# A decoder trunk in split float32 on one core: activations held still and weights moved 512 wide, with PE transposes between

## The chip, the cores and the metric

The kernel runs on one core of one Trainium2 chip. The metric is the device time of one execution in microseconds, from the first to the last instruction of the core with what the runtime measures around them; three runs of the kernel before are given, and one execution of it was taken with the hardware profiler. TensorE is written PE here, its weight loads PEld, VectorE DVE, ScalarE ACT, GpSimd POOL and SyncE SP, as in the profile.

## The reference

256 tokens of width 2048 pass through two layers. Every sublayer computes `h = h + RMSNorm_post(f(RMSNorm_pre(h)))`. With all gains and norms written `n()`:

```python
# layer 0
proj = n(h) @ w_in                        # 2048 x 6144: xin | C | B
h = h + n((B * conv3(C * xin)) @ w_out)   # causal depthwise convolution, width 3
h = h + n(square(relu(n(h) @ w_up0)) @ w_down0)      # 2048 x 8192, 8192 x 2048
K, V = split(n_kv(h) @ w_kv)              # 2048 x 4096, 16 heads of 128
# layer 1: stick-breaking attention, strictly causal, then the same MLP
z = q k / sqrt(128);  A = exp(log_sigmoid(z) + sum of log(1 - sigmoid(z)) over later keys)
h = h + n((A @ V) @ w_o)
h = h + n(square(relu(n(h) @ w_up1)) @ w_down1)
```

All inputs and the output are float32. The weights are 402.7 MB, which at 128 x 128 numbers a tile is 6144 tiles: 768 in `w_in`, 256 each in `w_out`, V, K, Q and `w_o`, 1024 in each half MLP matrix (up or down).

## The kernel before

**Precision.** PE multiplies in a reduced float32 format (`F32R`). Each operand is therefore split into a high part, rounded by an ACT copy, and a low part, the difference, made by DVE. A product is hi x hi + hi x lo + lo x hi.

**Layout.** Activations are kept transposed: features on partitions, the 256 tokens along a row. A weight tile of 128 x 128 is the stationary operand. `mm` (L211) needs two matmuls for a tile: the high part of the weights against 512 columns (256 tokens high, 256 tokens low, L218), and the low part against 256 columns (L219). The two halves of the 512-wide PSUM bank are added later by `combined` (L236: an ACT copy and a DVE add). In the last output column of a sublayer (`direct`, L213 to L217) three matmuls of 256 columns take their place, so that no such addition is needed at the end.

**Order.** `product` runs over the 16 (or 32) feature tiles of one output column; `products_lead` runs 6 or 7 output columns side by side at the start of a sublayer, so that PE can begin as soon as the first feature tile is ready. The V projection alone is done the other way (L497 to L511): the activations are stationary, the weights move 512 wide, in three matmuls for each pair (L509, L510, L511).

**Weights.** `load_one` brings chunks of 8 tiles (512 KB) on SP's queue into 4 buffers; `split_one` splits a chunk with one ACT copy (L173) and one DVE subtraction (L175) into one of 3 buffers for each part. 768 chunks are used in a fixed order; a chunk is split two ahead of its use.

**Between sublayers.** The sum of squares is gathered as tiles appear (`Squares`). At the end, `rstd_soon` (L294) makes the reciprocal root: matmuls with `pick` (L299), ACT square root (L304), DVE reciprocal and two diagonal matrices (L309), and matmuls that spread it over partitions (L313). Then `residual` (L342: L351, L353) updates `h` tile by tile, and `split_scaled` (L245: L247, L248) makes the next operand. PE can do nothing in that time, because the norm covers all 2048 features of a token.

**Attention.** Heads go in pairs. For each head there are float32 products: `scores` (L539, L540), the cumulative sums in `weights` (L572 to L577, in F32R), and `mixed` (L589, L590). They are placed by hand between the K and Q products of the following heads (L608 to L620). ACT has to load a function table when it changes between exp and log (L534). PSUM banks are given out in turn from one pool of 8.

The Tile framework's scheduler orders the instructions of each engine by priority, and inserts the semaphores.

Of the kernel before, what the change touches and what calls it, by code (L numbers as in the profile page):

```python
# [14 lines left out]
P = 128  # L15
D = 2048
T = 256
KD = D // P
FF = 4 * D
NF = FF // P  # L20
# [3 lines left out]
LEAD_UP = 7  # L24
CH = 8
FIRST = 2


def lead_then_rows(n_tiles, k_tiles, lead):
    """Order of weight tiles: the first `lead` columns k by k, the others column by column."""  # L30
    order = [(k, n) for k in range(k_tiles) for n in n_tiles[:lead]]
    order += [(k, n) for n in n_tiles[lead:] for k in range(k_tiles)]
    return order


IN_N = [j * KD + i for i in range(KD) for j in range(3)]
HALF = NF // 2

ORDERS = {
    "in": lead_then_rows(IN_N, KD, LEAD),  # L40
    "out": lead_then_rows(list(range(KD)), KD, LEAD),
    "v": [(k, KD + 8 * g + n) for g in range(2) for k in range(KD) for n in range(8)],
    "kq": [(k, n) for n in range(KD) for k in range(KD)],
    "wo": lead_then_rows(list(range(KD)), KD, LEAD),
    "up0": lead_then_rows(list(range(HALF)), KD, LEAD_UP),
    "up1": lead_then_rows(list(range(HALF, NF)), KD, 0),
    "dn0": [(k, n) for n in range(KD) for k in range(HALF)],
    "dn1": [(k, n) for n in range(KD) for k in range(HALF, NF)],
}

G_MIX0, G_POST0, G_MLP0, G_MPOST0, G_KV, G_MIX1, G_POST1, G_MLP1, G_MPOST1, G_C0, G_C1, G_C2 = range(12)
# [3 lines left out]
def trunk(ctx, tc, xT, vecs, ws, outT):  # L55
    nc = tc.nc
    const = ctx.enter_context(tc.tile_pool(name="const", bufs=1))
    res = ctx.enter_context(tc.tile_pool(name="res", bufs=KD // 2))
    act = ctx.enter_context(tc.tile_pool(name="act", bufs=48))
    wpool = ctx.enter_context(tc.tile_pool(name="w", bufs=4))  # L60
    wsplit = ctx.enter_context(tc.tile_pool(name="ws", bufs=3))
    tmp = ctx.enter_context(tc.tile_pool(name="tmp", bufs=3))
    psum = ctx.enter_context(tc.tile_pool(name="ps", bufs=8, space=bass.MemoryType.PSUM))

    gv = const.tile([P, 12, KD], F32, name="gv")
    nc.scalar.dma_start(gv[:], vecs.rearrange("p (g k) -> p g k", g=12))

    def g(i, k):
# [6 lines left out]
    pick = const.tile([P, 3], F32, name="pick")  # L75
    nc.vector.memset(pick[:], 0.0)
    nc.vector.memset(pick[:, 1:2], 1.0 / D)
    ones = const.tile([P, P], F32, name="ones")
    nc.vector.memset(ones[:], 1.0)
    later = const.tile([P, P], F32, name="later")  # L80
    nc.gpsimd.affine_select(
        out=later[:], in_=ones[:], pattern=[[-1, P]], compare_op=ALU.is_gt,
        fill=0.0, base=0, channel_multiplier=1,
    )
    causal = const.tile([P, P], F32, name="causal")
    nc.gpsimd.affine_select(
        out=causal[:], in_=ones[:], pattern=[[1, P]], compare_op=ALU.is_gt,
        fill=0.0, base=0, channel_multiplier=-1,
    )

    ident = const.tile([P, P], F32, name="ident")
    nc.gpsimd.affine_select(
        out=ident[:], in_=ones[:], pattern=[[1, P]], compare_op=ALU.is_equal,
        fill=0.0, base=0, channel_multiplier=-1,
    )
# [6 lines left out]
    def bank(name):  # L102
        return psum.tile([P, 512], F32, tag="ps", name=name)

    def small(tag, name=None, bufs=3, cols=T):
        return tmp.tile([P, cols], F32, tag=tag, name=name or tag, bufs=bufs)

    # ---- weights: a stream of chunks of CH tiles, each split exactly into two parts
    stream = []

    class Weights:
        def __init__(self, name, ap):
            self.ap, self.order = ap, ORDERS[name]
            self.at = {kn: i for i, kn in enumerate(self.order)}
            self.n = ap.shape[0]
            self.got = {}
            stream.extend((self, c) for c in range(self.n))

        def parts(self, k, n):
            i = self.at[(k, n)]  # L120
            ahead((self, i // CH))
            hi, lo = self.got[i // CH]
            return hi[:, i % CH, :], lo[:, i % CH, :]

        def wide(self, k, n):
            i = self.at[(k, n)]
            ahead((self, i // CH))
            hi, lo = self.got[i // CH]
            j = i % CH
            return (  # L130
                hi[:, j : j + 4, :].rearrange("p a b -> p (a b)"),
                lo[:, j : j + 4, :].rearrange("p a b -> p (a b)"),
            )

    state = {"loaded": 0, "split": 0, "limit": 1 << 30, "order": (None, None)}
    raw = {}

    def load_one():
        i = state["loaded"]
        if i >= len(stream):  # L140
            return
        w, c = stream[i]
        t = wpool.tile([P, CH, P], F32, tag="raw", name=f"raw{i}")
        n = CH // 2 if i < FIRST else CH
        for a in range(0, CH, n):
            nc.sync.dma_start(
                t[:, a : a + n, :], w.ap[c, :, a * P : (a + n) * P].rearrange("p (a b) -> p a b", a=n)
            )
        raw[i] = t
        state["loaded"] += 1  # L150

    def after(ins):
        return nullcontext() if ins is None else tc.issue_after(ins.ins)

    def urgent(w):
        return tc.high_priority() if w in kq.values() else nullcontext()

    def split_one():
        hi_after, lo_after = state["order"]
        i = state["split"]  # L160
        if i >= len(stream):
            return
        while state["loaded"] <= i:
            load_one()
        w, c = stream[i]
        t = raw.pop(i)
        hi = wsplit.tile([P, CH, P], F32R, tag="hi", name=f"whi{i}")
        lo = wsplit.tile([P, CH, P], F32R, tag="lo", name=f"wlo{i}")
        n = 2 if i < FIRST else CH
        for a in range(0, CH, n):  # L170
            at = slice(a, a + n)
            with after(hi_after), urgent(w):
                nc.scalar.activation(hi[:, at, :], t[:, at, :], AF.Copy)  # L173
            with after(lo_after), urgent(w):
                nc.vector.tensor_tensor(lo[:, at, :], t[:, at, :], hi[:, at, :].bitcast(F32), op=ALU.subtract)  # L175
        w.got[c] = (hi, lo)
        state["split"] += 1
        load_one()

    done = set()  # L180

    def ahead(key):
        if key in done:
            return
        done.add(key)
        i = stream.index(key)
        while state["split"] <= min(i + 2, state["limit"]) and state["split"] < len(stream):
            split_one()

    def hold(name):  # L190
        """Until the next norm is under way, split no more than two chunks after this phase."""
        state["limit"] = max(i for i, (w, _) in enumerate(stream) if w is W[name]) + 2

    W = {}
    sequence = ["in", "out", "up0_0", "dn0_0", "up1_0", "dn1_0", "v", "kq", "wo",
                "up0_1", "dn0_1", "up1_1", "dn1_1"]
    kq = {}
    for name in sequence:
        base = name[:3] if name[:2] in ("up", "dn") else name
        if name == "kq":  # L200
            K = Weights("kq", ws["k"])
            Q = Weights("kq", ws["q"])
            del stream[-2 * K.n :]
            for c in range(K.n):
                stream.extend([(K, c), (Q, c)])
            kq["k"], kq["q"] = K, Q
        else:
            W[name] = Weights(base, ws[name])

    # ---- building blocks  # L210
    def mm(ps, w, x, first, last, direct=False):  # L211
        hi, lo = w
        if direct:  # L213
            nc.tensor.matmul(ps[:, :T], hi, x[:, :T], start=first, stop=False)  # L214
            nc.tensor.matmul(ps[:, :T], hi, x[:, T:], start=False, stop=False)  # L215
            nc.tensor.matmul(ps[:, :T], lo, x[:, :T], start=False, stop=last)  # L216
            return  # L217
        nc.tensor.matmul(ps[:], hi, x[:], start=first, stop=False)  # L218
        nc.tensor.matmul(ps[:, :T], lo, x[:, :T], start=False, stop=last)  # L219

    def product(w, xs, n, ks, direct=False):
        ps = bank("acc")
        for i, k in enumerate(ks):
            mm(ps, w.parts(k, n), xs[k], i == 0, i == len(ks) - 1, direct)
        return ps

    def products_lead(w, xs, ns, ks, before=None):
        pss = [bank("lead") for _ in ns]
        for i, k in enumerate(ks):
            if before is not None:  # L230
# [469 lines left out]
```

## Time and profile before

| | |
|---|---|
| Time, median of 3 runs | 2214.81 us (2212.7, 2214.81, 2215.17) |
| Span of the profiled execution | 2212.8 us; no time of its own is given beside the span |
| Mean granted PE clock | 0.993 |
| PE busy | 99% of the span, 12492 matmuls |
| DVE, ACT busy | 65%, 51% |
| DMA | 409.04 MB, 185 GB/s |

Busy time of PE is modelled, and neighbouring matmuls overlap in it: a share of 99% says that PE always had a matmul in flight, not that it was at its peak. The pace is read from the starts of neighbouring matmuls. A row of a group gives: line, engine, operation, tiles, shapes, count, then busy us, mean ns of one, idle time before and its releasers.

### The profile page before, as it was taken

What the parts mean: (1) busy time and instruction counts of PE and PEld (TensorE: products, weight loads), DVE (VectorE), ACT (ScalarE), POOL (GpSimd) and SP (SyncE); (2) the same over time, 40 slices, a digit from 0 to 9 for tenths busy, and PEclk for the clock granted to TensorE, in tenths of its full rate; (3) what the DMA queues carried; (4) which work ended last, traced back from release to release, by engine and by line L of the source; (5) the groups of instructions that cost most, each with busy time, mean ns of one, the idle gap of its engine ahead of it and who ended that gap; (6) DMA issues with size and microseconds to landing.
All of it is one profiled execution on the core that took longest, in us unless ns stands there. A gap on an engine that the chain in (4) does not pass through costs nothing.

```text
span 2212.8 us, 31971 instructions
## 1 busy us (share of the span) xinstructions
PE 2180.2 (99%) x12492; PEld 1910.6 (86%) x12492; DVE 1440.5 (65%) x2100; ACT 1119.9 (51%) x1630; POOL 1.0 (0%) x7
## 2 busy tenths in 40 slices
PE   8999999999999999999999999999999999999997
PEld 7888888888888888888888888888888888888886
DVE  7766656977444677655675777669775446776555
ACT  6444455544444444444465666656544444444442
POOL 0000000000000000000000000000000000000000
PEclk9999999999999999999999999999999999999998
DMA  6555554555555555555455444445555555555553
GB/s 240 191 190 190 191 190 162 190 191 190 190 190 191 189 191 189 191 189 190 167 190 182 163 164 163 167 163 190 190 190 190 190 190 190 189 190 190 190 189 120
DMA packets 113480, 409.04 MB, mean 185 GB/s; under 512 B 12592, under 2 KB 12720, under 8 KB 113328
## 3 DMA queue, kind: packets, MB, share of 16 engines
q1 hardware_dynamic: 112608, 405.85, 54.1%
q8 instruction: 98, 1.61, 0.3%
q10 hardware_dynamic: 720, 1.15, 0.1%
q14 instruction: 54, 0.44, 0.1%
HBM read 404.85 MB, written 2.10 MB: 184 GB/s over the span
## 4 chain that ended last, share of the span: by engine, by line
PE 98%; DVE 1%; ACT 0%; DMA 0%; issue 0%; ACTq 0%; DVEq 0%
PE acc L218 55%; PE acc L219 28%; PE lead L218 6%; PE lead L219 3%; PE accv L509 1%; PE accv L511 1%; PE accv L510 1%; PE acc L216 1%; PE acc L214 1%; PE acc L215 1%; PE z L539 0%; DVE x L353 0%; PE o L589 0%; DVE upd L351 0%; DMA gv<-vecs 0%; PE ex L572 0%
## 5 line engine op out<-in xcount | busy, mean ns | idle before, releaser
L218 PE MATMUL acc<-u,whi 128*128 128x512 f32 x5136 | 1786.3, 393 | 0.0
L219 PE MATMUL acc<-u,wlo 128*128 128x256 f32 x5136 | 1429.9, 278 | 0.0
L175 DVE TENSOR_TENSOR wlo<-raw,whi 128x1024 fp32r<-128x1024 f32 (+1 forms) x774 | 940.7, 1216 | 710.2 <-ACT whi L173 709.5
L173 ACT ACTIVATE whi<-raw 128x1024 fp32r<-128x1024 f32 (+1 forms) x774 | 814.7, 1053 | 1002.4 <-PE acc L218 486.1
L218 PEld LDWEIGHTS acc<-u,whi 128*128 128x128 f32 x5136 | 962.2, 187 | 218.6
L219 PEld LDWEIGHTS acc<-u,wlo 128*128 128x128 f32 x5136 | 966.6, 188 | 0.2
L218 PE MATMUL lead<-u,whi 128*128 128x512 f32 x416 | 151.5, 407 | 10.9 <-ACT whi L173 6.6
L219 PE MATMUL lead<-u,wlo 128*128 128x256 f32 x416 | 119.0, 286 | 0.0
L218 PEld LDWEIGHTS lead<-u,whi 128*128 128x128 f32 x416 | 81.4, 196 | 30.0 <-ACT whi L173 6.6
L238 ACT ACTIVATE half<-acc 128x256 f32<-128x256 f32 x268 | 97.7, 364 | 0.0
L240 DVE TENSOR_TENSOR sum<-acc,half 128x256 f32<-128x256 f32 x204 | 85.1, 417 | 0.1
L219 PEld LDWEIGHTS lead<-u,wlo 128*128 128x128 f32 x416 | 81.8, 197 | 0.2 <-DVE wlo L175 0.2
L256 DVE TENSOR_TENSOR u<-sum,u 128x256 fp32r<-128x256 f32 x144 | 59.1, 418 | 0.0
L255 ACT ACTIVATE u<-sum 128x256 fp32r<-128x256 f32 x144 | 56.6, 402 | 1.9 <-DVE sum L441 1.8
L441 DVE SCALAR_TENSOR_TENSOR sum<-sum 128x256 f32<-128x256 f32 x128 | 53.8, 423 | 3.7
L440 DVE TENSOR_TENSOR sum<-sum,rstd 128x256 f32<-128x256 f32 x128 | 53.5, 423 | 3.7
L509 PE MATMUL accv<-whi,u 128*128 128x512 f32 x128 | 50.7, 396 | 1.5 <-ACT u L247 1.5
L218 PE MATMUL acc<-o,whi 128*128 128x512 f32 x144 | 50.9, 399 | 0.0
L511 PE MATMUL accv<-whi,u 128*128 128x512 f32 x128 | 50.3, 393 | 0.0
L510 PE MATMUL accv<-wlo,u 128*128 128x512 f32 x128 | 50.3, 393 | 0.0
L270 DVE TENSOR_TENSOR acc<-acc,sq 128x256 f32<-128x256 f32 (+1 forms) x84 | 42.7, 508 | 9.0 <-ACT sq L278 8.7
L247 ACT ACTIVATE u<-x,gv 128x256 fp32r<-128x256 f32 x80 | 36.0, 498 | 14.7 <-DVE x L353 11.5
(116 smaller groups left out, 949.2 us busy)
## 6 DMA issues: line engine op xcount, KB each, us to landing
raw<-w_up SPq DMA_DIRECT2D x256, 512.0 KB, 4.2
raw<-w_dn SPq DMA_DIRECT2D x256, 512.0 KB, 4.2
raw<-w_in SPq DMA_DIRECT2D x94, 512.0 KB, 3.2
raw<-w_out SPq DMA_DIRECT2D x32, 512.0 KB, 3.2
raw<-w_v SPq DMA_DIRECT2D x32, 512.0 KB, 3.3
raw<-w_k SPq DMA_DIRECT2D x32, 512.0 KB, 3.3
raw<-w_q SPq DMA_DIRECT2D x32, 512.0 KB, 3.3
raw<-w_wo SPq DMA_DIRECT2D x32, 512.0 KB, 3.3
```

Of the source, the lines that this page charges most:

```text
L173: nc.scalar.activation(hi[:, at, :], t[:, at, :], AF.Copy)
L175: nc.vector.tensor_tensor(lo[:, at, :], t[:, at, :], hi[:, at, :].bitcast(F32), op=ALU.subtract)
L218: nc.tensor.matmul(ps[:], hi, x[:], start=first, stop=False)
L219: nc.tensor.matmul(ps[:, :T], lo, x[:, :T], start=False, stop=last)
L238: nc.scalar.activation(b[:], ps[:, T:], AF.Copy)
L240: nc.vector.tensor_tensor(s if out is not None else s[:], ps[:, :T], b[:], op=ALU.add)
L255: nc.scalar.activation(u[:, :T], x[:], AF.Copy)
L256: nc.vector.tensor_tensor(u[:, T:], x[:], u[:, :T].bitcast(F32), op=ALU.subtract)
L441: nc.vector.scalar_tensor_tensor(s[:], s[:], 0.0, s[:], op0=ALU.max, op1=ALU.mult)
L509: nc.tensor.matmul(pss[b][c][:], xh, hi, start=k == 0, stop=False)
L510: nc.tensor.matmul(pss[b][c][:], xh, lo, start=False, stop=False)
L511: nc.tensor.matmul(pss[b][c][:], xl, hi, start=False, stop=k == KD - 1)
```

## The change

The first projection (`w_in` and the convolution) stays as it is. In all other sublayers the roles of the operands change: 128 tokens x 128 features of the activations are stationary, and the weights move 512 columns at a time. The 256 tokens become two blocks `b` of 128. A `unit` is the work of one chunk for one block: two output pieces of 512 columns, three matmuls each. The second block runs `LAG = 4` units behind the first, in the same PE order; the last four units of a sublayer are regrouped (`tail`). Results now have tokens on partitions, so that a norm is a per-partition scalar, but the next product needs features on partitions again: `transposed` turns four 128 x 128 tiles by PE transposes into PSUM, and `operand_from` splits them. PE's order is written by hand (`manual_schedule`), with a heap of delayed calls counted in units (`at`, `tick`). The ring of split weights grows from 3 to 7 buffers. PSUM banks are named: in attention 0 to 3 are for K, Q and V, 4 and 5 for `z`, and 6 and 7 for everything else. The gains before K, V and Q are multiplied into the weights when these are split, by a per-partition scale (two pieces of 512 in a chunk of K or Q).

```diff
+LAG = 4
+RING = 7
+AHEAD = 2
...
+        gains = w.gains(c) if w.gains else [None] * (4 if i < FIRST else 1)
+                nc.scalar.activation(hi[:, at], t[:, at], AF.Copy, scale=gain)
...
+    def transposed(src, to):
+        for j in range(4):
+            nc.tensor.transpose(to[:, j * P : (j + 1) * P], src[:, j * P : (j + 1) * P], ident[:])
+        return to[:].rearrange("p (k t) -> p k t", k=4)
+    def operand_from(src, x4, b, to):
+        t = transposed(src, to)
+        hi, lo = x4[:, :, 0, b, :], x4[:, :, 1, b, :]
+        nc.scalar.activation(hi, t, AF.Copy)
+        nc.vector.tensor_tensor(lo, t, hi.bitcast(F32), op=ALU.subtract)
...
+        def half(self, b, c, i):                       # Group: one piece of a unit
+                nc.tensor.matmul(ps[:], xh, hi[:, a], start=i == 0 and k == 0, stop=False)
+                nc.tensor.matmul(ps[:], xh, lo[:, a], start=False, stop=False)
+                nc.tensor.matmul(ps[:], xl, hi[:, a], start=False, stop=i == self.n - 1 and k == self.ks - 1)
...
+    def run(groups):
+        units = [(gr, i) for gr in groups for i in range(gr.n)]
+        n = len(units)
+        for t in range(n + LAG):
+            for b, j in ((0, t), (1, t - LAG)):
+                if not 0 <= j < n:
+                    continue
+                gr, i = units[j]
+                (gr.tail if j >= n - LAG else gr.unit)(b, i)
+                tick()
...
+        def finish(self, b):                           # Norms: h += mg * rstd, then the next operand
+                r = inverse_root(self.ss[b][:, 3:4], self.bias[b][:])
+                for c in range(4):
+                    nc.vector.scalar_tensor_tensor(
+                        piece(h[b], c), self.mg[b][c], r[:], piece(h[b], c), op0=ALU.mult, op1=ALU.add)
+                    if self.last:
+                        eng.dma_start(piece(out[b * P : (b + 1) * P, :], c), piece(h[b], c))
+                        continue
+                        nc.vector.tensor_tensor(u, piece(h[b], c), piece(self.gpre, c), op=ALU.mult)
+                    at(LAG + c, lambda b=b, c=c, u=u: self.enter(b, c, u))
...
+        def hidden(xs):                                # MLP: after an up group
+            def evict(b, c, ps):
+                nc.scalar.activation(s[:], ps[:], AF.Relu, scale=before.hs[b][:])
+                nc.scalar.activation(s[:], s[:], AF.Square)
+                at(3 + c % 2, enter)                   # enter: operand_from(s, xs[c], b, tbank())
...
+    def abank(name):
+        kind = "z" if name == "z" else "other"
+        rot[kind] += 1
+        return bank((4 if kind == "z" else 6) + rot[kind] % 2, name)
...
+        at(5, lambda: scores(pair(a)))                 # attention beside the next K and Q
+        at(8, lambda: log_sigmoids(pair(a)))
+        at(20, lambda: weights(pair(a)))
+        at(27, lambda: mix(a))
```

The products of attention (`scores`, `weights`, `mixed`) keep their instructions. `combined`, `rstd_soon`, `residual` and `products_lead` are gone outside the first projection. The output leaves with tokens on rows, as each piece of `h` is finished.

More of the change, by code (lines that the diff above doesn't have):

```diff
@@ L197, in trunk @@
[L197 to L219, printed above, removed]
```

905 lines of the change are left out of this document (453 added, 452 removed).

## The prediction

> **What bounds the kernel now.** I read the page's engine shares and its chain first, then the stages.
>
> ```profile
> PE 2180.2 (99%) x12492; PEld 1910.6 (86%) x12492; DVE 1440.5 (65%) x2100; ACT 1119.9 (51%) x1630; POOL 1.0 (0%) x7
> PE 98%; DVE 1%; ACT 0%; DMA 0%; issue 0%; ACTq 0%; DVEq 0%
> q1 hardware_dynamic: 112608, 405.85, 54.1%
> ```
>
> PE is 98% of the chain that ended last, and DMA is about half used: only PE's own pace, its gaps and the end can change the time. The weights in these 405.85 MB stay the same, on the same queue; the 8 MB that the change adds (`x` by tokens, six rows of gains, both on POOL's queue) find the other half free, and I cost them at nothing. The view by windows, cut at the sublayers, gives the terms (columns: window, length, busy PE, PEld, DVE, ACT, POOL with counts, granted clock, DMA share, GB/s):
>
> ```profile
> 0.00:276.10 276.10, 269.46 (x1537) 235.59 (x1538) 194.18 (x309) 140.59 (x208) 1.03 (x7) 1.00 0.58 201
> 276.10:365.30 89.20, 89.20 (x532) 78.69 (x531) 52.09 (x68) 49.32 (x79) 0.00 (x0) 1.00 0.54 189
> 370.67:1083.50 712.83, 712.83 (x4132) 624.55 (x4133) 450.83 (x613) 340.40 (x469) 0.00 (x0) 1.00 0.55 189
> 1088.27:1178.60 90.33, 90.33 (x395) 74.78 (x396) 66.57 (x91) 55.86 (x87) 0.00 (x0) 0.98 0.53 181
> 1178.60:1383.20 204.60, 204.12 (x1176) 178.72 (x1175) 149.60 (x273) 132.13 (x211) 0.00 (x0) 1.00 0.48 167
> 1383.20:1476.50 93.30, 93.30 (x549) 82.05 (x548) 59.64 (x95) 57.58 (x95) 0.00 (x0) 1.00 0.52 177
> 1481.90:2195.50 713.60, 713.60 (x4133) 630.18 (x4133) 448.33 (x611) 338.09 (x467) 0.00 (x0) 1.00 0.56 185
> ```
>
> They are: first projection; `w_out`; MLP 0; V; K and Q with attention; `w_o` with attention's rest; MLP 1. Between them lie three gaps (365.30 to 370.67, 1083.50 to 1088.27, 1476.50 to 1481.90; 15.5 us) and at the end 17.3 us.
>
> **The pace.** The old form is read from a long window of PE alone, the new one from V, which has it already: the same three matmuls, one weight load each. Starts in the timeline give the pace, since durations overlap.
>
> ```profile
> 450.00:1050.00 600.00, 600.00 (x3464) 1.00 0.56 190
> ...
> 1151.74 0.39 PE L511 MATMUL accv<-whi,u 128*128 128x512 f32 x1
> ...
> 1153.10 0.39 PE L511 MATMUL accv<-whi,u 128*128 128x512 f32 x1
> ```
>
> 3464 matmuls in 600 us, two for each tile, are 0.3464 us a tile. The two accv rows lie six matmuls apart: 1.36 / 6 = 0.2267 us. Four tiles need six such, so a tile costs 1.5 x 0.2267 = 0.340 us. The old 256-wide matmul takes 0.3464 - 0.2267 = 0.120 us, more than half of the 512-wide one: about 0.013 us is fixed in each matmul, and there are 1.5 instead of 2 for a tile. By stage, at 0.340 us a tile (the rows hold also the `direct` columns, norm matmuls and slow-clock starts):
> - `w_out`, 256 tiles: 89.2 to 87.0, saves 2.2.
> - MLP 0, 2048 tiles: 712.8 to 696.3, saves 16.5; MLP 1: 713.6 to 696.3, saves 17.3.
> - V, 256 tiles: 90.3 to 87.0, saves 3.3 (its slow start).
> - K, Q, `w_o`, 768 tiles: 204.6 + 93.3 = 297.9, of which 261.1 remain for the tiles; attention's own products follow below.
>
> **Attention's float32 products, and what a transpose costs.** No PE transpose is in this trace. The nearest rows are float32 matmuls of 128 x 128 and weight loads for a 1-wide matmul:
>
> ```profile
> 1133.60 0.63 PEld L489 LDWEIGHTS rtok<-mean,acc 128*128 128x128 f32 x4
> ...
> 1238.08 0.59 PE L589 MATMUL o<-lb,mg 128*128 128x256 f32 x2
> 1238.51 0.38 PE L590 MATMUL o<-lb,mg 128*128 128x128 f32 x2
> 1238.73 0.60 PE L589 MATMUL o<-lb,mg 128*128 128x256 f32 x2
> ...
> L590 PE MATMUL o<-lb,mg 128*128 128x128 f32 x32 | 6.1, 274 | 0.0
> ```
>
> From 1238.08 to 1238.73 a head's `mixed` takes 0.65 us, `scores` has the same shapes, and `weights` is 512 + 256 + 256 columns at the F32R pace, 0.47: 16 x 1.77 = 28.3 us, unchanged. So K, Q and `w_o` come to 289.4 and save 8.5.
>
> A float32 matmul appears as two records (16 products, x32). The L590 pair takes 0.22 us, 0.11 each. Four loads for 1-wide matmuls take 0.63 us; without the last load's own 0.19, and the 0.22 of the 256-wide pass before (half of the 0.43 between the first L589 and L590), two steps of 0.11 remain. So neither a pass of 128 columns nor a weight load comes faster than 0.11. I take one record a transpose, since the moving operand is an identity, whose parts below the first are zero: 0.112 us, the load's pace. The order of the changed program has 416 transposes in 104 blocks of four: 104 x 0.448 = 46.6 us, all on PE. Ends: 0.066 us by the F32R slope (0.0127 + 128 x 0.00042), 27 us in all; 0.22 us with two records, 93 us.
>
> [...]
>
> **Gaps.** Half-clock starts follow each gap: rows of a window behind each.
>
> ```profile
> 1476.69 0.29 PE L216 MATMUL acc<-o,wlo 128*128 128x256 f32 x1
> 1476.81 0.50 PE L299 MATMUL ms<-pick,acc 128*128 128x2 f32 x4
> ...
> 1481.89 0.76 PE L218 MATMUL lead<-u,whi 128*128 128x512 f32 x1 [2.12 <-DVE u L248]
> ...
> 370.60:380.00 9.40, 9.33 (x43) 8.15 (x44) 7.93 (x13) 6.16 (x11) 0.00 (x0) 0.79 0.29 98
> 1088.20:1098.00 9.80, 9.72 (x36) 7.93 (x37) 8.58 (x14) 6.78 (x12) 0.00 (x0) 0.84 0.32 109
> 1481.80:1491.80 10.00, 9.91 (x43) 8.61 (x44) 7.83 (x13) 6.05 (x10) 0.00 (x0) 0.72 0.28 97
> ```
>
> The norm is serial for all 256 tokens today, and the clock means 0.79, 0.84 and 0.72 show part of each restart at half rate (about 2.0, 1.6 and 2.8 us lost, already in the stages). Afterwards block 0's norm lies behind three units of block 1 (3 x 1.36 = 4.1 us) before its first transpose is next on PE. The chain to cover is of these lengths:
>
> ```profile
> L278 ACT ACTIVATE sq<-x 128x512 f32<-128x512 f32 x32 | 19.7, 616 | 0.0
> L351 DVE TENSOR_TENSOR upd<-mg,ms 128x512 f32<-128x512 f32 x28 | 19.0, 680 | 0.0
> L175 DVE TENSOR_TENSOR wlo<-raw,whi 128x1024 fp32r<-128x1024 f32 x766 | 937.7, 1224 | 710.2 <-ACT whi L173 709.5
> L173 ACT ACTIVATE whi<-raw 128x1024 fp32r<-128x1024 f32 x766 | 812.0, 1060 | 1002.4 <-PE acc L218 486.1 <-issue 405.1 <-PE lead L218 58.2
> ```
>
> Square 0.62, root and reciprocal about 0.45, one or two updates and the gain at 0.68 each, hand-overs 0.4: 3 to 4 us, and a split of 1.06 or 1.22 may be in front. It nearly fits, the clock should not fall, and I leave 2 us for each place: 15.5 to 6, saves 9.5. If nothing covered it, the 15.5 us and the slow starts would stay.
>
> **End.** DVE updates eight pairs of tiles today and the last transfer goes out after 2209.65:
>
> ```profile
> 2208.96 0.69 DVE L353 TENSOR_TENSOR x<-x,upd 128x512 f32<-128x512 f32 x1
> ```
>
> Of the 17.3 us, 3.15 lie behind that row. Afterwards only block 1 is left: add 0.68, square 0.62, root and reciprocal 0.45, four updates 2.9, hand-overs 0.4, transfer 3.15: 8.2 us, saves 9.1.
>
> **New waits in attention.** Here I choose most. First, banks 6 and 7 carry transposes, `ex`, `ey` and `o`. In `weights` the second head's `ex` needs the bank that DVE is still reading for the first, and all units behind it on PE wait:
>
> ```profile
> L579 DVE TENSOR_TENSOR lb<-lb,ex 128x256 f32<-128x256 f32 x32 | 13.2, 414 | 6.2 <-PE ex L573 6.2
> L580 DVE TENSOR_TENSOR lb<-lb,ey 128x128 f32<-128x128 f32 x32 | 8.9, 278 | 0.0
> ```
>
> Two L579 and one L580 are 1.11 us, with latency 1.35: eight times 11 us, more if a split stands in front.
>
> Second, ACT. Per four heads and 16 chunks now, and the prices:
>
> ```profile
> 1230.00:1282.00 52.00, 52.00 (x301) 45.67 (x300) 40.01 (x77) 34.30 (x57) 0.00 (x0) 1.00 0.47 163
> ...
> L238 ACT ACTIVATE half<-acc 128x256 f32<-128x256 f32 x268 | 97.7, 364 | 0.0
> L534 ACT ACT_TABLE_LOAD x17 | 21.8, 1283 | 0.3
> L247 ACT ACTIVATE u<-x,gv 128x256 fp32r<-128x256 f32 x80 | 36.0, 498 | 14.7 <-DVE x L353 11.5 <-DMA gv<-vecs 2.3 <-DMA x<-xT 0.6
> L255 ACT ACTIVATE u<-sum 128x256 fp32r<-128x256 f32 x144 | 56.6, 402 | 1.9 <-DVE sum L441 1.8
> ```
>
> A per-partition scale costs 0.10 us (498 against 402), so a 512-wide piece is about 0.71. In the changed order four heads have ten table loads instead of four (+7.7), 32 split pieces of 0.71 instead of 16 of 1.06 (+5.8), eight copies around the transposes (+5.3), and lose eight `half` (-2.9): 34.3 + 15.9 = 50.2 us, where PE's work is 32 units x 1.36, four heads x 1.77 and four blocks x 0.448, 52.4 together. ACT is 96% booked and takes its queue in order: behind a run of three table loads and their functions (some 5.4 us) stands the split of the next chunk. The second block's lag holds five of the seven buffers, so its lead is two chunks (5.4 us) less its own 1.06 + 1.22. That is a stall of 2 to 3 us at some of the eight pairs; I take 12 us. Ends: none, and 5 us at each, 40. DVE, with 40.01 of 52, has room. In the MLPs ACT and DVE are near half busy and the bursts fit into the lead, so I cost those evictions at nothing; without it 64 blocks could each lose part of a microsecond.
>
> **Sum.** Gains 2.2 + 16.5 + 17.3 + 3.3 + 8.5 + 9.5 + 9.1 = 66.4. Losses 46.6 + 11 + 12 = 69.6. Span 2212.8 + 3.2 = 2216.0. The runs shown have a median 2.0 above that span: **2218 us**. A change under 0.2% (4.4 us) can hardly be told from none, so this is a draw with more room above; its own range, 2204 to 2234, takes in the bounds of gaps and waits.
>
> **Rivals.**
> - **Faster: the handwritten slots work.** ACT's bursts fall where the ring is full, and the gaps vanish: 12 + 6 us less, 2200. For: ACT still has 4% room, DVE more. Against: the table loads. Chance 0.30.
> - **Slower: each float32 transpose is two records.** The place is `transposed`, the price 416 x 0.112 more, 2265. For: all float32 matmuls in this trace are two. From 0.15 us a transpose on, the run is slower even with the slots working. Chance 0.12.
> - **Slower: transposes do not overlap**, 0.274 us each: 416 x 0.162 more, 2285. Against: L590's pace. Chance 0.03.
> - **Slower: ACT becomes the bound in attention**, 40 instead of 12 us: 2246. For: 96%. Chance 0.15.
> - **The fixed part of a matmul is not saved.** The V rows show this form at its pace; 36 us would be lost. I fold this into the slow cases.
>
> **Chances.** Forecast 0.40, of which 0.08 falls faster by over 0.2%, 0.12 within and 0.20 slower. With the rivals: faster 0.38, same 0.12, slower 0.50. The range 2193 to 2262 leaves out the two transpose rivals and a little of the fast side.
>
> **What would show it.** Right: starts of neighbouring 512-wide matmuls 0.227 apart in all sublayers, transposes as 416 records 0.11 apart, no slow-clock windows after the first, idle time before PE rows of `weights` and of units behind table loads. Wrong: 832 records; a transpose spacing near 0.07 or 0.2; PE idle in the MLPs before transposes; no idle time in attention.

## The result and the profile after

The changed kernel takes 2234.84 us (median of 4 runs, 2234.66 to 2235.2) against 2214.99 us of the kernel before (2212.7 to 2216.88): the ratio is 1.0091, 95% interval 1.0076 to 1.0105. It is slower by 20 us, or 0.9%: inside the range (2193 to 2262), and 17 us above the forecast of a draw. The profiled execution took 2234.89 us with a span of 2233.2 us, against a span of 2212.8 us before: +20.4, where the sum had +3.2.

The page of the changed kernel, its engines and its chain:

```profile
PE 2188.6 (98%) x10194; PEld 1818.7 (81%) x10194; DVE 1227.6 (55%) x1490; ACT 1149.3 (51%) x1492; POOL 5.4 (0%) x15
PE 94%; ACT 3%; DVE 2%; issue 1%; DMA 0%; SPq 0%; DVEq 0%; ACTq 0%
```

The chain gives the first hint: PE's share fell from 98% to 94% of a longer span, and ACT and DVE, nearly absent before, have 5% together, over 100 us of steps in which PE's next instruction hung on a split, a copy or an addition. Not all of that is loss, but the loss is in there. The view by windows follows. Its first three rows and its last are first projection, `w_out`, MLP 0 and MLP 1, as before. The three between are cut differently, because the changed kernel makes V in two halves: the fourth row is V's first half with the first K and Q, the fifth the other K and Q with attention, V's second half and the start of `w_o` (its first matmul is at 1401.6), the sixth the rest of `w_o`.

```profile
0.00:279.30 279.30, 271.47 (x1541) 235.87 (x1541) 198.75 (x312) 145.22 (x213) 2.18 (x9) 1.00 0.65 213
279.30:371.40 92.10, 88.88 (x387) 72.54 (x386) 45.01 (x51) 37.51 (x49) 1.06 (x2) 0.98 0.59 188
371.40:1091.00 719.60, 713.66 (x3219) 589.78 (x3217) 365.49 (x353) 342.20 (x402) 0.53 (x1) 1.00 0.60 189
1091.00:1184.00 93.00, 92.80 (x423) 76.63 (x424) 55.11 (x80) 56.15 (x89) 0.00 (x0) 0.98 0.57 176
1184.00:1430.00 246.00, 232.38 (x1078) 191.89 (x1078) 154.77 (x291) 194.60 (x296) 1.06 (x2) 0.99 0.51 160
1430.00:1504.00 74.00, 72.77 (x325) 59.73 (x324) 39.47 (x46) 33.53 (x45) 0.00 (x0) 1.00 0.57 184
1504.00:2220.00 716.00, 712.09 (x3212) 588.86 (x3211) 360.52 (x347) 338.37 (x398) 0.53 (x1) 1.00 0.59 185
```

Busy PE is short of the window by 3.2 us in the second row, 5.9 in the third, 13.6 in the fifth and 3.9 in the last; before, no row but the first and the fifth (0.5) was short at all, and its three gaps lay between the rows. No single place holds the loss. The places, from the groups of PE's instructions by line and from the timeline:

```profile
L198 PE MATMUL acc<-whi,y 128*128 128x512 f32 x128 | 50.9, 398 | 2.5 <-DVE sum L385 2.0 <-ACT whi L126 0.5
L159 PE MATMUL tr<-ident,s 128*128 128x128 f32 x256 | 38.3, 272 | 0.0
L159 PE MATMUL tr<-ident,hg 128*128 128x128 f32 x64 | 9.7, 274 | 5.4 <-DVE bias L282 3.5 <-DVE hg L300 1.9
L581 PE MATMUL ex<-gone,later_r 128*128 128x512 f32 x16 | 7.0, 439 | 13.3 <-DVE lb L588 13.3
```

```profile
279.18 0.40 PE L200 MATMUL acc<-whi,y 128*128 128x512 f32 x1
281.56 0.50 PE L198 MATMUL acc<-whi,y 128*128 128x512 f32 x1 [1.99 <-DVE sum L385]
...
356.56 0.39 PE L200 MATMUL acc<-whi,y 128*128 128x512 f32 x1
357.42 0.50 PE L198 MATMUL acc<-whi,y 128*128 128x512 f32 x1 [0.47 <-ACT whi L126]
358.68 0.50 PE L199 MATMUL acc<-wlo,y 128*128 128x512 f32 x1 [0.76 <-DVE wlo L127]
...
608.60 0.39 PE L200 MATMUL acc<-whi,u 128*128 128x512 f32 x1
608.84 0.60 PE L159 MATMUL tr<-ident,s 128*128 128x128 f32 x4
...
609.50 0.40 PE L199 MATMUL acc<-wlo,u 128*128 128x512 f32 x1
...
1223.73 0.28 PE L586 MATMUL ey<-gone,later_r 128*128 128x256 f32 x1
1226.22 0.47 PE L581 MATMUL ex<-gone,later_r 128*128 128x512 f32 x1 [2.20 <-DVE lb L588]
```

A step of 512 columns without a wait is 0.227 us from start to start, so what lies above it is lost. Read from top to bottom:
- `w_out` starts in banks 0 and 1, and the last column of the first projection is still being added up there on DVE, behind a split: 2.38 between starts, 2.15 lost, and a stretch at half clock (granted 0.50 for 3.41 us) behind it.
- The `tail` of `w_out` wants the last chunk two steps early: 0.86 and 1.26 between starts, 1.67 lost, and the same two numbers again behind the matmuls at 1076.58, 1489.41 and 2209.43.
- A block of four transposes of hidden values: 608.60 to 609.50 is 0.90 where two steps would be 0.45. It costs 0.45, and PE never waits ahead of it (idle 0.0 in the L159 row of `s`).
- The second head of `weights` waits for DVE to read the bank of the first: 2.48 between starts here, eight such waits of 1.3 to 2.48.

At the start the `h` loads on POOL's queue take their part of the DMA engines. DMA issues of the first 20 us, the changed kernel and then the kernel before (count, KB each, median us to landing):

```profile
h<-x POOLq DMA_DIRECT2D x2, 1024.0 KB, 7.6
x<-xT SPq DMA_DIRECT2D x5, 256.0 KB, 9.3
```

```profile
x<-xT SPq DMA_DIRECT2D x6, 256.0 KB, 5.1
```

The first operands take 4 us longer to land; the last matmul of the first projection starts at 278.61 instead of 276.15, 2.5 us later.

### The profile page after: what moved, and what is told of

It reads as the page before. It is cut to its first block, busy times and chain, and to the rows that moved or that the text cites. A ratio compares the mean times of both kernels' runs of the same rounds, so it can differ in the third digit from the quotient of the medians.

```text
span 2233.2 us, 26716 instructions
## 1 busy us (share of the span) xinstructions
PE 2188.6 (98%) x10194; PEld 1818.7 (81%) x10194; DVE 1227.6 (55%) x1490; ACT 1149.3 (51%) x1492; POOL 5.4 (0%) x15
## 4 chain that ended last, share of the span: by engine, by line
PE 94%; ACT 3%; DVE 2%; issue 1%; DMA 0%; SPq 0%; DVEq 0%; ACTq 0%
PE acc L199 27%; PE acc L200 27%; PE acc L198 26%; PE acc L378 7%; PE acc L379 3%; PE tr L159 2%; PE lead L378 1%; ACT whi L129 1%; DVE wlo L127 1%; ACT whi L126 1%; PE lead L379 0%; DMA x<-xT 0%; DVE wlo L130 0%; ACT L543 0%; PE o L598 0%
## 5 line engine op out<-in xcount | busy, mean ns | idle before, releaser
L198 PE MATMUL acc<-whi,u 128*128 128x512 f32 x1408 | 556.6, 395 | 0.0
L200 PE MATMUL acc<-whi,u 128*128 128x512 f32 x1408 | 549.5, 390 | 0.0
L199 PE MATMUL acc<-wlo,u 128*128 128x512 f32 x1408 | 549.0, 390 | 0.3
L198 PE MATMUL acc<-whi,hid 128*128 128x512 f32 x1024 | 401.5, 392 | 0.9 <-ACT whi L126 0.9
L199 PE MATMUL acc<-wlo,hid 128*128 128x512 f32 x1024 | 399.3, 390 | 1.5 <-DVE wlo L127 1.5
L200 PE MATMUL acc<-whi,hid 128*128 128x512 f32 x1024 | 399.2, 390 | 0.0
L200 PEld LDWEIGHTS acc<-whi,u 128*128 128x128 f32 x1408 | 264.6, 188 | 55.8
L198 PEld LDWEIGHTS acc<-whi,u 128*128 128x128 f32 x1408 | 265.0, 188 | 52.1
L378 PE MATMUL acc<-u,whi 128*128 128x512 f32 x672 | 233.2, 394 | 0.0
L198 PEld LDWEIGHTS acc<-whi,hid 128*128 128x128 f32 x1024 | 192.6, 188 | 40.9 <-ACT whi L126 1.8
L200 PEld LDWEIGHTS acc<-whi,hid 128*128 128x128 f32 x1024 | 192.5, 188 | 40.1
L379 PE MATMUL acc<-u,wlo 128*128 128x256 f32 x672 | 186.2, 277 | 0.0
L378 PEld LDWEIGHTS acc<-u,whi 128*128 128x128 f32 x672 | 126.0, 187 | 29.2
L379 PEld LDWEIGHTS acc<-u,wlo 128*128 128x128 f32 x672 | 126.2, 188 | 0.0
```

Of the source, the lines that this page charges most:

```text
L198: nc.tensor.matmul(ps[:], xh, hi[:, a], start=i == 0 and k == 0, stop=False)
L199: nc.tensor.matmul(ps[:], xh, lo[:, a], start=False, stop=False)
L200: nc.tensor.matmul(ps[:], xl, hi[:, a], start=False, stop=i == self.n - 1 and k == self.ks - 1)
L378: nc.tensor.matmul(ps[:], hi[:, s], xs, start=first, stop=False)
L379: nc.tensor.matmul(ps[:, :T], lo[:, s], xs[:, :T], start=False, stop=last)
```

## The experiments

**The two heads of `weights` apart.** The wait in front of L581 is the largest. Giving each head of a pair its own slot takes away what makes it wait, one head's bank.

```diff
-            at(7, lambda: weights(pair(a - 1)))
+            at(7, lambda: weights((a * 2 - 2,)))
+            at(9, lambda: weights((a * 2 - 1,)))
...
-        at(20, lambda: weights(pair(a)))
+        at(20, lambda: weights((2 * a,)))
+        at(22, lambda: weights((2 * a + 1,)))
...
```

> The two heads of a pair get their cumulative sums (weights) two units apart, so that the bank of the first head's ex has 2.7 us in which DVE can read it; nothing else moves. Theory (banks 6 and 7 are the wait): the 13.3 us that PE stands idle before L581 fall to under 2 us and the half-clock stretch after 1283 goes, so the span falls by 13 to 15 us, to about 2219. Rival (ACT is late, and DVE's queue waits behind it, whatever the banks): the idle time moves to the units that need the next split weights, and the span falls by less than 5 us.

Measured: span 2231.9, 2234.25 us. Groups on PE of this kernel:

```profile
L159 PE MATMUL tr<-ident,tk 128*128 128x128 f32 x64 | 10.7, 294 | 5.5 <-ACT tk L615 4.2 <-DVE lb L588 1.3
L581 PE MATMUL ex<-gone,later_r 128*128 128x512 f32 x16 | 6.2, 390 | 0.0
```

L581 went from 13.3 to 0.0, and the time stayed: 5.5 us of waiting came back before the transposes of K and Q, some 4 before units (0.72 to 2.34 between starts), and there are three half-clock stretches in attention instead of one. The bank was the place of the wait; the rows now name ACT and DVE, whose lateness the wait for the bank had hidden.

**`w_out` away from the last banks of the first projection.**

```diff
-    state = {"pair": 0, "t": 0}
+    state = {"pair": 1, "t": 0}
```

> The pairs of banks start with 2 and 3 instead of 0 and 1, so that the first unit of the output projection does not need a bank that the last columns of the first projection still hold. Theory: the gap at 279.2 (2.4 us between starts) and the half-clock stretch behind it go: 3.5 to 4 us less. Rival (the gap is the operand y or the weights of the first chunk): it stays, and less than 1 us is gained.

Measured: span 2233.1, 2233.92 us. The gap at 279 and its stretch are gone and everything up to attention is 3.7 us earlier (the last L200 before block 0's transposes for V starts at 1084.86 instead of 1088.60). Then attention has four half-clock stretches (from 1222, 1280, 1338 and 1393) instead of one. Its waits are the same, 1.30 to 2.48, and by the tail of `w_o` the 3.7 us are used up (1489.38 and 1489.41). Why an equal wait costs 1.7 us more in one run than in another is taken up at the end.

**`x` by tokens behind the weights on SP's queue.**

```diff
-            nc.gpsimd.dma_start(h[b][:], x[b * P : (b + 1) * P, :])
+            nc.sync.dma_start(h[b][:], x[b * P : (b + 1) * P, :])
```

> The two loads of x by tokens (1 MB each) go out on SP's queue behind the first operands instead of on the POOL queue at the start. Theory (they share the transfer engines with the first weights and xT): the first projection ends 3 us earlier and the span falls by 2.5 to 3.5 us. Rival (the start is slow for another reason): no change within 1 us.

Measured: span 2228.3, 2231.44 us. The last matmul of the first projection starts at 275.15, 3.5 us earlier than in the changed kernel and 1.0 earlier than in the kernel before. The term is real. The rest of the 4.9 us of span is one half-clock stretch fewer.

**A tail of two units instead of four.**

```diff
-            p = i - (self.n - LAG)
-            c, j = p // 2, p % 2 * 2 + self.n - LAG
-            self.half(b, c, j)
-            self.half(b, c, j + 1)
-            if p % 2:
-                self.evict(b, c, self.ps.pop((b, c)))
+            c = i - (self.n - 2)
+            self.half(b, c, self.n - 2)
+            self.half(b, c, self.n - 1)
+            self.evict(b, c, self.ps.pop((b, c)))
...
-                (gr.tail if j >= n - LAG else gr.unit)(b, i)
+                (gr.tail if j >= n - 2 else gr.unit)(b, i)
```

> Only the last two units of a sublayer are regrouped by output piece instead of the last four, so that the last chunk is needed one step earlier than in order instead of two. Theory (the regrouping runs ahead of the ring of split weights): each of the four places with starts 0.86 and 1.26 us apart shrinks from 1.7 us to under 0.6, and the span falls by 3 to 6 us, less what the norm then waits for the earlier piece's square. Rival (the norm's chain decides these places): what is gained there comes back before the transposes, no change within 1 us or a loss of up to 3.

Measured: span 2242.0, 2242.63 us; the span is 8.8 longer. The tails' waits of 0.86 and 1.26 are gone, and the norm, which now begins later, pushes the splits aside. Timeline of PE in this kernel:

```profile
380.82 0.80 PE L199 MATMUL acc<-wlo,u 128*128 128x512 f32 x1 [3.91 <-DVE wlo L127]
```

The waits at the boundaries (4.39 here, 4.05 before V and 4.39 before MLP 1) take back what the tails gave. The rest goes with the clock: the half-clock stretches between 100 and 2150 us add up to 30.7 us instead of 10.2. So the tail of four is worth its waits of 1.67: at this boundary DVE, which makes the split, comes last.

**Function tables loaded in turn.** The logarithms of a pair are kept behind the exponentials of the pair before.

```diff
-            nc.scalar.activation(lb[:], lb[:], AF.Exp)
+            held["exp"] = nc.scalar.activation(lb[:], lb[:], AF.Exp).ins
...
     def log_sigmoids(hds):
+        with tc.issue_after(held["exp"]) if "exp" in held else nullcontext():
...
```

> Keeps on ACT the logarithms of a pair behind the exponentials (of weights) that come before them in the program, so that the function tables are loaded in turn: 19 loads in attention instead of 38, about 24 us less on ACT (19 x 1.28). Theory (ACT's lateness sets when DVE reaches the adds behind ex, and the two banks set the rest): idle time of PE before L581 falls from 13.3 to about 8, since the waits of 2.5 become the 1.3 of two adds and their latency, the half-clock stretch behind them goes, span -6 to -9, near 2225. Rival (the two banks alone make the wait, whatever ACT does): idle before L581 stays at 13, span within 1.5 of 2233.2. Second rival, from the run with the heads apart: the wait only moves to the transposes of K and Q and to units; idle before L581 falls and the span stays.

Measured: span 2232.8, 2233.91 us. Table loads on ACT in the changed kernel, and then in this one with its L582 (the L581 of the changed kernel):

```profile
L543 ACT ACT_TABLE_LOAD x17 | 21.8, 1283 | 0.3
L564 ACT ACT_TABLE_LOAD x11 | 14.1, 1283 | 0.2
L590 ACT ACT_TABLE_LOAD x10 | 12.8, 1283 | 0.1
```

```profile
L543 ACT ACT_TABLE_LOAD x17 | 21.8, 1283 | 0.3
L565 ACT ACT_TABLE_LOAD x1 | 1.3, 1283 | 0.0
L591 ACT ACT_TABLE_LOAD x1 | 1.3, 1283 | 0.0
L582 PE MATMUL ex<-gone,later_r 128*128 128x512 f32 x16 | 7.2, 449 | 12.9 <-DVE lb L589 12.9
```

Nineteen loads, 24 us of ACT, are gone and the wait is 12.9 instead of 13.3. The first rival is right: while the bank is in front, ACT's load hardly moves this wait.

**Without the transposes of the hidden values.** It leaves out 256 of the 416 transposes; the operand is split from the hidden values as they lie, so the products are no longer those of the reference; the engines' work stays.

```diff
-                    operand_from(s, xs[c], b, tbank())
+                    t = s[:].rearrange("p (k t) -> p k t", k=4)
+                    hi, lo = xs[c][:, :, 0, b, :], xs[c][:, :, 1, b, :]
+                    nc.scalar.activation(hi, t, AF.Copy)
+                    nc.vector.tensor_tensor(lo, t, hi.bitcast(F32), op=ALU.subtract)
```

> Leaves out the 256 transposes of the hidden values of the two MLPs (the operand is split straight from the hidden values as they lie); ACT and DVE keep the same instructions from SBUF instead of PSUM. Theory (a block of four costs 0.447 us of PE and nothing else): 64 x 0.447 = 28.6 us less, span 2204.6, give or take 2. Rival (a block also makes the following matmuls slow or holds PE's queue, the 0.23 pace behind blocks): 64 x 0.52 = 33 us less, 2200. Rival (the evictions are what PE waits for and the transposes lie in that time): under 20 us less, over 2213.

Measured: 2207.52 us (6 runs), 27.3 less; span 2206.7. The same stretch of MLP 0, from the last transposes before it to its tail, in windows of the changed kernel and of this one:

```profile
379.22:1076.58 697.36, 696.40 (x3142) 576.60 (x3141) 348.30 (x326) 328.27 (x375) 0.00 (x0) 1.00 0.60 190
```

```profile
379.04:1061.38 682.34, 681.39 (x3014) 564.00 (x3013) 347.08 (x326) 326.44 (x375) 0.00 (x0) 1.00 0.63 194
```

15.02 us for 32 blocks is 0.469 a block, and MLP 1 gives the same 15.02. At that price all 104 blocks cost 48.8 us, an estimate, since 64 of them were left out. The price lies between the theory (0.447) and its rival (0.52), near the theory. The MLPs gain 30.0 us and the span only 26.5: there are five half-clock stretches before the end instead of three, four of them in attention, which this edit does not touch.

**Three units of lag, three chunks of lead.**

```diff
-LAG = 4
+LAG = 3
+TAIL = 4
-AHEAD = 2
+AHEAD = 3
```

> Block 1 runs three units behind instead of four, and the freed buffer of split weights goes to the lead: three chunks ahead instead of two; the regrouped end keeps four units. Theory (what is late is the lead of two chunks: splits in front of the norm's work, and splits late behind tables): the waits of 0.86 and 1.26 in the four tails vanish (-6.7), attention's waits of 2.5 become 1.3 (-5 with the half-clock stretch), and the norm boundaries, with one unit less of cover, stay near 10: span about 2221. Rival (the norm's own chain decides): six boundaries take 1.36 more each, 8.2 in all, and half-clock stretches with them; tails -6.7, span 2233 to 2240.

Measured: span 2235.7, 2237.03 us. The tails' waits vanish, but in the groups on PE (one line number higher here)

```profile
L160 PE MATMUL tr<-ident,hg 128*128 128x128 f32 x64 | 10.2, 283 | 6.7 <-DVE hg L301 6.7
L160 PE MATMUL tr<-ident,tk 128*128 128x128 f32 x64 | 9.8, 275 | 3.1 <-ACT tk L616 1.6 <-DVE o L155 1.5
```

the boundaries before the MLPs wait 6.7 instead of 5.4 and K and Q's transposes 3.1 instead of 0.0. The rival is right, for the reason that the shorter tail gave: at a boundary the norm's chain, not the lead, is what comes last.

**Together.** Tables in turn, heads apart (slots 6 and 8, 19 and 21), the `h` loads on SP, `w_out` on other banks, and a third bank for transposes, `ex`, `ey` and `o`, K and Q making do with three:

```diff
-            banks = [[(2 * n + b) % 4] for b in range(NB)]
+            banks = [[(2 * n + b + 2) % 3] for b in range(NB)]
...
-        return bank((4 if kind == "z" else 6) + rot[kind] % 2, name)
+        if kind == "z":
+            return bank(4 + rot[kind] % 2, name)
+        return bank([6, 7, 3][rot[kind] % held["others"]], name)
...
```

> Together: tables loaded in turn; the two heads of weights one or two units apart; a third bank (3) for transposes, ex, ey and o while K and Q run (K and Q on three banks instead of four); x by tokens on SP's queue behind the first weights; w_out's accumulators away from the last banks of the first projection. Theory (each removes its own wait: start and first gap -4.9, the 279 gap in that, attention's waits of 15.5 and 1.7): first projection ends near 275.7, attention without waits over 0.5, span near 2233.2 - 4.9 - 2.4 - 16 = 2210, 0.998 of the time before. Rival (a wait goes to the next place where ACT or DVE is late, as with the heads apart): attention keeps half of its waits and two or more half-clock stretches, span 2218 to 2226. Tails and norm boundaries stay as they are in both.

Measured: 2219.54 us (6 runs), ratio to before 1.0028 (1.0015 to 1.004); span 2216.7. Up to the first tail it gains 8.0 us, from there to the tail of `w_o` 8.4. The second number is more than the heads apart (1.3) and the tables (0.4) gave one by one. That these waits hide one another fits it, but is not shown: the third bank was not tried alone, and could be the larger part. The groups on PE:

```profile
L584 PE MATMUL ex<-gone,later_r 128*128 128x512 f32 x16 | 6.2, 390 | 0.0
L159 PE MATMUL tr<-ident,tk 128*128 128x128 f32 x64 | 10.1, 281 | 2.3 <-DVE lb L591 2.3
L198 PE MATMUL acc<-whi,o 128*128 128x512 f32 x128 | 50.8, 397 | 4.5 <-DVE lm L572 4.0 <-ACT whi L126 0.5
```

One new wait of 4.0 is of my making: I had given `w_o` the banks of the scores, which DVE still read.

**The gains in the weights.** With that bank choice mended, the gains before the MLPs are multiplied into the up weights at the split, so `hg` leaves DVE.

```diff
-            W["up", i, q] = Weights(ws[f"up{i}{q}"])
+            W["up", i, q] = Weights(ws[f"up{i}{q}"], k_gains(G_MLP0 + i, 1))
...
-        return pool, Norms(pool, row(pool, post, "gpost"), row(pool, pre, "gpre"))
+        return pool, Norms(pool, row(pool, post, "gpost"))
...
```

> As the kernel with all changes together, and two more: the output projection no longer takes the banks of the scores (its first unit waited 4.38 for DVE to read them), and the gains before the MLPs are multiplied into the up weights when these are split, as for K, Q and V, so that the 16 multiplications hg (0.68 each) leave DVE at the two boundaries before the MLPs. Theory (DVE's work of a block, five pieces of 0.68 for each of four columns beside a split of 1.22 for every 2.72 us, sets the waits at the boundaries): 4.4 + 1.7 us go in attention, the waits of 2.16 and 1.3 before the first transposes of both MLPs fall to 1 and 0.5, -4: span near 2206.5. Rival (the boundary's waits are of the same length without hg, as before V, where there is none: 2.39 + 0.44 + 0.89): only the bank counts, span 2210 to 2211.

Measured: 2208.42 us (8 runs), ratio to before 0.9973 (0.9962 to 0.9983). From the tail of `w_out` to that of MLP 0 it takes 717.1 us where the kernel with all changes together took 720.0, and MLP 1 gains as much. Attention gains 6.7: the wait of the bank, 4.38 between starts, and two half-clock stretches are gone. In the timeline the waits of 2.16 and 1.3 before MLP 0 have become steps without a wait and one of 0.42. Groups on PE (now `h` stands for `hg` too):

```profile
L159 PE MATMUL tr<-ident,h 128*128 128x128 f32 x96 | 14.5, 273 | 3.0 <-DVE h L290 2.9
```

The theory held, but only where `hg` was: before V, where there was none, the wait is 2.71 between starts (2.39 in the changed kernel).

**The same with three units of lag.** The edit is that of the run with this lag alone.

> The same with block 1 three units behind instead of four and three chunks ahead instead of two. Theory (with DVE relieved at the boundaries the lead is worth more than the cover): tails -6.7, boundaries +1 each against the run beside it, span near 2203. Rival (what the run with this lag alone showed: waits of about 1 us before four of the K and Q transposes, boundaries of 4.1 instead of 3.5): -6.7 + 4.7 + 2, span the same as the run beside it, within 2 us.

Measured: 2208.65 us (10 runs). The rival is right: the tails' 6.7 us are gained, and paid back at the boundaries (waits of 2.32 to 2.83 between starts), in attention (two of 0.97) and in two half-clock stretches.

**The last chunks split in halves.**

```diff
-        gains = w.gains(c) if w.gains else [None] * (4 if i < FIRST else 1)
+        gains = w.gains(c) if w.gains else [None] * (4 if i < FIRST else 2 if i in last_two else 1)
...
```

> As the kernel with the gains in the weights (block 1 four units behind), and the last two chunks of the four sublayers that end in a regrouped tail (w_out, both MLPs, w_o) are split in two pieces of 512 columns each instead of one of 1024. Theory (a tail waits 0.63 for the high part of the last chunk and 1.03 for its low part, because the ring buffer comes free only one unit before; the first half is ready 0.46 and 1.0 sooner): starts of 0.86 and 1.26 in the four tails become about 0.4 and 0.5, 4 us in all, so about 2204.5 against 2208.4 of the kernel with the gains in the weights, and 0.995 of the kernel before. Rival (the pieces' fixed costs and hand-overs on ACT and DVE make the norm behind the tail late by as much): within 1 of 2208.4.

Measured: 2204.66 us (5 runs), ratio to before 0.9959 (0.9945 to 0.9972); this version is faster than the kernel before by 0.4%, and than the changed kernel by more. The tail of `w_out` in its timeline:

```profile
348.86 0.39 PE L200 MATMUL acc<-whi,y 128*128 128x512 f32 x1
349.29 0.50 PE L198 MATMUL acc<-whi,y 128*128 128x512 f32 x1
350.01 0.50 PE L199 MATMUL acc<-wlo,y 128*128 128x512 f32 x1 [0.22 <-DVE wlo L127]
```

0.43 and 0.72 instead of 0.86 and 1.26: 0.97 a tail, and the other three tails show the same steps: 3.9 in all. The medians differ by 3.8, on different chips: beside these runs the kernel before took 2213.66, beside the others 2215.23, and by the two ratios the gain is 3.1. The traces show the gain more surely than the times do.

## Why the prediction came out as it did

The direction with the larger chance came true and the time lies in the range, but the forecast itself, a draw, was off by 17 us. Both are in part luck: 0.30 of the chance of slower came from three rivals (two records a transpose, no overlap, ACT as the bound), the range reached beyond 2234 for the sake of the last, and none of them came true. The loss came from places that the sum had at nothing or too small. Term by term:
- **Pace, right.** Starts are 0.227 apart in all sublayers; MLP 0 without its hidden transposes is 682.34 us for 3014 recorded matmuls, 0.2264 each. The tiles' gains by stage, 2.2 to 17.3 us, follow from this pace.
- **Transposes, right.** 416 records, 0.109 apart, with a mean duration of 271 to 292 ns; 46.6 predicted, 48.8 by the run without the hidden ones. The two rivals on transposes fall. The duration is near the 274 of the L590 row, but the price on PE is 0.109: pricing them by that row's pace of 0.11 and not by its 274 was the right step. The reason I gave for one record was an argument of mine: the runs show the one record, not why it is one.
- **End, right.** The last matmul starts at 2224.16 and the span ends 9.0 later; 8.2 predicted.
- **Attention, 23 predicted, 16.3 measured** (14.6 between starts and 1.7 of half clock), with a wrong split: the bank term, 11, was the whole of it, and ACT's 12 did not show, because the wait for the bank gave ACT the time. Once the bank was free, waits for ACT appeared, as the run with the heads apart shows (4.2 before the transposes of K and Q). The two terms are rivals for the same time, and I added them. The count of ACT's work was right, 48 to 50 us for four heads, but these took 58 us; with 24 us of table loads gone the time stayed.
- **Boundaries, 6 predicted, 10.3 measured** (8.6 between starts and 1.7 of half clock). The step that failed is the length of the chain. I took 3 to 4 us of latency from one column's operations; before the MLPs DVE has four columns of them, beside the splits. Windows of the changed kernel behind `w_out` and in the middle of MLP 0, and the rows of two waits, before MLP 0 and before V:

```profile
371.00:383.00 12.00, 9.29 (x50) 7.29 (x49) 11.95 (x21) 10.34 (x25) 0.53 (x1) 1.00 0.59 208
700.00:1000.00 300.00, 300.00 (x1352) 248.46 (x1352) 147.72 (x134) 137.18 (x150) 0.00 (x0) 1.00 0.61 190
...
374.09 0.40 PE L200 MATMUL acc<-whi,u 128*128 128x512 f32 x1
375.42 0.68 DVE L300 TENSOR_TENSOR hg<-h,gpre 128x512 f32<-128x512 f32 x1
376.25 0.63 PE L159 MATMUL tr<-ident,hg 128*128 128x128 f32 x4 [1.76 <-DVE bias L282]
...
1087.54 1.28 DVE L130 SCALAR_TENSOR_TENSOR wlo<-raw,gv,whi 128x1024 fp32r<-128x1024 f32 x1 [0.84 <-ACT whi L129]
1088.60 0.39 PE L200 MATMUL acc<-whi,hid 128*128 128x512 f32 x1
1090.98 0.63 PE L159 MATMUL tr<-ident,h 128*128 128x128 f32 x4 [2.00 <-issue]
```

Before MLP 0 DVE is busy for 11.95 of 12 us, and half of the time elsewhere. Block 0's first three columns are in time; its fourth is late. The count was to be had beforehand: up to that column's transposes DVE has one product, four updates, four gains and three low parts of block 0 and two products of block 1, 14 x 0.68 = 9.5 us, and two splits of 1.22: 12.0 us, where PE is there for them after 9.4 (from 364.9, the end of block 0's products, to 374.3). Taking `hg` out of it removed the wait, which shows it. Before V it is otherwise: the first column is late, DVE is busy for only 9.4 of the 14 us from 1077 on, and its idle 0.84 lies within the chain. There one column's latency is what counts, with a split in front of its add, of its square on ACT and of its reciprocal: 6.0 us, from 1084.9 to 1090.9, where PE is there after 3.9 (at 1088.8). No run changed that chain alone.
- **Costed at nothing: start, 2.5.** "The other half free" is true of the mean (54.1% on SP's queue) and not of the first 20 us, where the share (the last column but one) is 0.84 in the kernel before already:

```profile
0.00:20.00 20.00, 13.36 (x61) 11.52 (x61) 13.49 (x33) 13.25 (x25) 1.03 (x7) 1.00 0.84 294
```

- **Costed at nothing: `w_out`'s first banks, 3.9** with the half clock; the run with other banks gained 3.7 there. I followed the bank rotation in attention and not at the join with the first projection.
- **Costed at nothing: tails, 6.7.** The regrouped tail was read as an order of work, and its need for the ring two steps early was not worked out: the buffer for the last chunk of `w_out` comes free at 356.3, half a microsecond before PE wants the chunk (356.8), and 1.06 + 1.22 of splitting follow.
- **Clock "should not fall", wrong:** three half-clock stretches of 3.41 us, about half of it, 1.7, lost in each (counted above with their waits).

Against the sum these make 2.5 + 3.9 + 6.7 + 4.3 + 2.2 (transposes) + 0.8 (end) - 6.7 (attention) = 13.7 of the 17.2 between forecast and profile. The other 3.5 us are not assigned to a place by any run.

## What to carry to other kernels

Before adding the prices of two waits, ask whether the second would still be late after the first; and where removing one wait brings nothing, remove the next together with it before calling it innocent. At a boundary, count an engine's whole work over all columns against the cover, and not only the latency of one column. A mean share of half, of DMA or DVE, says nothing about the 10 us in which everything falls together (here 0.84 of DMA in the first 20 us, and 11.95 of 12 us of DVE before MLP 0): cut a window there.

## What was not expected of the hardware

**Whether a wait cost half-clock time went with where it fell.** The same wait of 2.48 between starts is followed by full clock at 1226 and 1341 and by half clock at 1283. Windows of the changed kernel behind the three waits:

```profile
1283.20:1286.60 3.40, 3.40 (x10) 2.72 (x11) 2.02 (x6) 1.68 (x2) 0.00 (x0) 0.50 0.51 165
1226.20:1229.60 3.40, 3.38 (x16) 2.88 (x17) 2.54 (x8) 2.88 (x5) 0.00 (x0) 1.00 0.58 172
1341.50:1344.90 3.40, 3.37 (x16) 2.84 (x17) 2.23 (x8) 3.06 (x5) 0.00 (x0) 1.00 0.52 171
```

Within a run all half-clock stretches begin whole multiples of 3.413 us apart (283.11, 1092.07 and 1283.22 in the changed kernel: 237 and 56 of them, and each lasts 3.41). I laid that grid over the eleven runs of the changed form that had a stretch between 100 and 2150 us, counting PE as idle, where starts lie over 0.5 us apart, from 0.4 us after the one until the next. Of the grid's steps at full clock, all 37 with over 1.9 us of idle time were followed by a step at half clock, and none of the 59 with 1.0 to 1.85 (between them one was, one was not). In the changed kernel alone, the steps ahead of its three stretches hold 1.86, 1.99 and 2.08 us, and eight steps with 1.02 to 1.80 have full clock behind them. So the wait of 2.48 before 1283, of which one step holds 2.08, cost 1.7 us more, and the two that two steps share (1.06 and 1.02 before 1226, 1.80 and 0.28 before 1341) cost nothing more. With 3.7 us saved early, in the run with `w_out` on other banks, the same waits of 1.30 to 2.48 met four stretches. This was read from the traces and not set up as a test. The twelfth run, with the gains in the weights, agrees: on the grid of its only stretch, at 2203.52 and so at the end, no step before 2150 us holds more than 1.87 us of idle time, and it has no stretch there, though two of its waits are 2.71 and 2.60 between starts.

**The first projection has two paces.** In the profiled execution of the kernel with the gains in the weights its matmuls start 0.1767 us apart on average between 60 and 270 us, in all other profiled executions 0.1733, at a granted clock of 1.00 in both: 5 us over that stage. It is the slowest of that kernel's eight runs. The cause is open.
